# Row maxima, output weights and latent roots placed anew in a hybrid attention and convolution block

## Chip, cores and metric

The kernel runs on one core of a Trainium2 chip. The metric is the device time of one execution in microseconds; the median of the runs counts. Engines are named TensorE (PE in the profile, its weight load PEld), VectorE (DVE), ScalarE (ACT), GpSimd (POOL) and SyncE (SP, which only issues transfers).

## What is computed

One layer of a streaming encoder on 1024 frames of width 1024, with 16 meta tokens ahead of them, and a final norm:

```
n = RMSNorm(h);  z = n @ W_in  ->  conv value | conv gate | c_q (384) | c_kv (256) | k_rot (32)
A: u = a * sigmoid(gate); causal depthwise conv, 31 taps; LayerNorm; swish
B: q = RMSNorm(c_q) @ W_uq;  k, v = RMSNorm(c_kv) @ W_ukv;  rotary on q and the shared k_rot;
   8 heads, softmax over visible chunks (64 frames a chunk, causal by chunk)
h += concat(RMSNorm(A), RMSNorm(B)) @ W_out
h += (silu(conv3(n2 @ W_up)) * conv3(n2 @ W_up)) @ W_down,  n2 = RMSNorm(h)
out = RMSNorm(h), meta tokens dropped
```

All of it is in float32. The kernel makes each float32 product from three TensorE products of a high and a low part: a value x is rounded to `hi` (float32r), `lo = x - hi`, and hi*hi + hi*lo + lo*hi are summed.

## The kernel before

The work is traced in one program; a scheduler orders each engine's instructions by a simulated timeline, with earlier traced work first among what is ready. Three kinds of blocks change this order: `manual_schedule` keeps the traced order on the engines named, `issue_after(x)` puts what is traced in it, on the engine of x, behind x, and `high_priority` puts its instructions ahead of others that are ready. Within an engine everything then runs in that order. 43 equal pages of on-chip memory are shared by weights, activations and heads.

Stages, in order of time:

- Norm of the input and its transposition, then the gated unit (`glu`) of the convolution's four channel groups. Each group's 31 taps (`conv31`, lines 300 to 308) run on VectorE as some 50 operations of 513 columns.
- The latents (class `Latent`): `multiply(g)` makes c_kv or c_q for a third of the rows (three tiles, one PSUM bank each) with ScalarE's squares behind it, and `normalize(g)` takes the root (`rsqrt`, line 173: ScalarE's square root, VectorE's reciprocal, one Newton step), scales the banks to `cn`, transposes, and splits into `cH` and `cL` (lines 505, 506). For the latents the Newton step runs on GpSimd (`eng=G`, lines 185 to 196). The key's rotary part is turned on GpSimd within `multiply` (lines 470 to 477), five operations for each third, and is transposed and split within `normalize`. Rotary products of the queries are in `rope` (line 423).
- Weights come through one list (`want`, `load`, `fetch`): SyncE loads `raw`, then `wh` is a copy (line 244 or 246) and `wl` GpSimd's subtraction (line 247). A block of w_out is first scaled by VectorE (line 242).
- `pair(0..3)` makes the queries and keys of two heads each; those of heads 2 to 7 are spilled to DRAM and loaded as heads (`load_head`, ten transfers; the masks are extra rows of `qh` and `kh`). SyncE issues all transfers, in order.
- `max_pass` makes the row maxima of a head: 15 products `smax` (line 645), each reduced by VectorE into `mp`, then one more reduction, a transposition, ScalarE's negated copy `mr` (line 653), and two transfers of it into row RM of `qh` (lines 654, 655). With that row the scores come out of TensorE already shifted.
- Attention runs over 120 units, 15 a head: `score(u)` makes three products and an exponential `p`, its copy `ph` and `pl = p - ph` on GpSimd or VectorE (line 681); `weigh(u)`, four units later, multiplies with the values. At each unit two steps of the next head's `max_pass` are taken, so a head's maxima are made in the first eight units of the head before it. At the first unit of heads 5, 6 and 7 two or three blocks of w_out are fetched. The convolution's LayerNorm (`conv_branch`) is put between, from unit 10 on.
- Then the output projection, the up-projection and the down-projection.

Of the kernel before, what the change touches and what calls it, by code (L numbers as in the profile page):

```python
# [10 lines left out]
F32 = mybir.dt.float32  # L11
# [8 lines left out]
P = 128  # L20
D = 1024
# [72 lines left out]
def block_kernel(ctx: ExitStack, tc: tile.TileContext, a: dict, out: bass.AP):  # L94
# [139 lines left out]
    def fetch(upto, eng=None):  # L234
        while issued[0] < min(upto, len(queue)):
            key, src, shape = queue[issued[0]]
            issued[0] += 1
            load(issued[0])
            raw = raws.pop(key)
            wh, wl = page("wh", shape, F32R), page("wl", shape, F32R)  # L240
            if key[0] == "out":
                V.tensor_scalar(raw, raw, outT[:, key[1]:key[1] + 1], None, ALU.mult)
            if eng is None:
                S.activation(wh, raw, AF.Copy)  # L244
            else:
                eng.tensor_copy(wh, raw)
            G.tensor_tensor(wl, raw, f(wh), ALU.subtract)  # L247
            ready[key] = (wh, wl)
# [174 lines left out]
    def rope(dst, ps, i, n, g):  # L423

        ta = ea("ropea", "ta", [P, g, 2, 16])
        tb = ea("ropeb", "tb", [P, g, 2, 16])
        cb = cosq[:n, i, :].unsqueeze(1).unsqueeze(1).broadcast_to([n, g, 2, 16])
        sb = sinq[:n, i, :].unsqueeze(1).broadcast_to([n, g, 16])
        V.tensor_tensor(ta[:n], ps, cb, ALU.mult)
        V.tensor_tensor(tb[:n, :, 0, :], ps[:, :, 1, :], sb, ALU.mult)  # L430
        V.tensor_tensor(tb[:n, :, 1, :], ps[:, :, 0, :], sb, ALU.mult)
        G.tensor_tensor(dst[:, :, 0, :], ta[:n, :, 0, :], tb[:n, :, 0, :], ALU.subtract)
        G.tensor_tensor(dst[:, :, 1, :], ta[:n, :, 1, :], tb[:n, :, 1, :], ALU.add)

    class Latent:
# [8 lines left out]
        def multiply(self, g, odd):  # L444
# [24 lines left out]
            if self.extra:  # L469
                ta, tb = ea("ropea", "ta", [P, 3, 2, 16]), ea("ropeb", "tb", [P, 3, 2, 16])  # L470
                cb = cosq[:, g0:g1, :].unsqueeze(2).broadcast_to([P, 3, 2, 16])
                sb = sinq[:, g0:g1, :]
                G.tensor_tensor(ta, kr, cb, ALU.mult)
                G.tensor_tensor(tb[:, :, 0, :], kr[:, :, 1, :], sb, ALU.mult)
                G.tensor_tensor(tb[:, :, 1, :], kr[:, :, 0, :], sb, ALU.mult)
                G.tensor_tensor(kr[:, :, 0, :], ta[:, :, 0, :], tb[:, :, 0, :], ALU.subtract)
                G.tensor_tensor(kr[:, :, 1, :], ta[:, :, 1, :], tb[:, :, 1, :], ALU.add)

        def normalize(self, g):
# [7 lines left out]
            rsqrt(r[:, :3], ss[:, :3], 1.0 / w, 3, root=True, eng=G)  # L487
# [4 lines left out]
            for k in range(nk + (1 if self.extra else 0)):  # L492
                rows = P if k < nk else DR
                if g == 0:
                    self.cH.append(page(self.name + "H", [rows, TP], F32R))
                    self.cL.append(page(self.name + "L", [rows, TP], F32R))
                pt = bank("tp")
                for i in range(g0, g1):
                    pos, n = KT[i]
                    src = cns[i - g0][:n, k * P:(k + 1) * P] if k < nk else krall[:n, i].rearrange("p x c -> p (x c)")  # L500
                    transpose(pt[:rows, pos - base:pos - base + n], src, n)
                hi, lo, ps = self.cH[k][:, base:end], self.cL[k][:, base:end], pt[:rows, :end - base]
                if k < nk:
                    gk = latT[:, goff + k:goff + k + 1]
                    S.activation(hi, ps, AF.Copy, scale=gk)
# [37 lines left out]
    def rot(g, odd):  # L543
        rts[g] = rot_multiply(g, odd)


    steps = [
# [3 lines left out]
        lambda: lcq.multiply(2, 1), lambda: lcq.normalize(1), lambda: rot(0, 0),  # L551
# [9 lines left out]
    qmask_d = dram.tile([NMASK, TP], F32, name="qmask_d")  # L561
    kmask_d = dram.tile([NMASK + 1, TP], F32, name="kmask_d")
    SY.dma_start(out=qmask_d, in_=a["qmask"])
# [28 lines left out]
    def load_head(h):  # L592
# [15 lines left out]
        SY.dma_start(out=f(qh)[DN + DR:RM, Q0:T], in_=qmask_d[:, Q0:T])  # L608
# [20 lines left out]
    def max_pass(tiles):  # L629
# [24 lines left out]
        SY.dma_start(out=f(qh)[RM:RM + 1, 16:T], in_=f(mr)[:8])  # L654
        shifts.append(SY.dma_start(out=f(qh)[RM:RM + 1, Q0:16], in_=f(mr)[8:9, :2]).ins)
# [6 lines left out]
    def score(u):  # L662
# [18 lines left out]
        (V if turn[0] % PLV[h] == 0 else G).tensor_tensor(pl[:n], p32[:n], f(ph)[:n], ALU.subtract)  # L681
# [4 lines left out]
    PLV = [4, 4, 4, 3, 3, 2, 2, 2]  # L686
# [82 lines left out]
    def conv_branch():  # L769
        lng = page("lng", [P, D])  # L770
        SY.dma_start(out=lng[:, :DC], in_=a["conv_ln_g"].partition_broadcast(P))
        SY.dma_start(out=lng[:, DC:], in_=a["conv_ln_b"].partition_broadcast(P))
# [285 lines left out]
    fill = iter(())  # L1058
# [258 lines left out]
```

## Time and profile before

| | |
|---|---|
| time, median of 3 runs | 1281.35 us (1278.2 to 1284.28) |
| the profiled execution's own time | 1281.71 us |
| its span, first to last instruction | 1279.9 us |
| mean granted TensorE clock | 0.976 |
| busy: PE, DVE, ACT, POOL | 1199.5, 904.4, 542.1, 333.7 us |

Busy times are sums over the whole span; matmuls overlap each other, so a busy PE is not PE at its peak. A row of a timeline has the start, the duration, engine, line and tiles (out<-in), and in brackets how long the engine was idle before and what ended that. A clock of 1.00 is 2.4 GHz; the other level is 1.2 GHz.

### The profile page before, as it was taken

How to read it: one execution, taken by the hardware profiler on the slowest of the kernel's cores; microseconds unless marked ns; L12 is line 12 of the kernel's file. 1: busy time of each engine (PE TensorE's matmuls, PEld its weight loads, DVE VectorE, ACT ScalarE, POOL GpSimd, SP SyncE). 2: the span in 40 equal slices, each digit the busy share in tenths (PEclk: the TensorE clock that was granted, in tenths of full speed). 3: DMA queues.
4: the chain of work that ended last, by engine and by line, in shares of the span. 5: the costliest groups of instructions: out<-in, count | busy, mean ns of one | idle time of the engine just before them, and what ended most of it. 6: DMA issues, size and time to landing. Idle time of an engine off the chain costs nothing.

```text
span 1279.9 us, 20327 instructions
## 1 busy us (share of the span) xinstructions
PE 1199.5 (94%) x7867; PEld 1105.6 (86%) x7867; DVE 904.4 (71%) x1600; ACT 542.1 (42%) x1049; POOL 333.7 (26%) x309
## 2 busy tenths in 40 slices
PE   7899779988997999997999999999999989999997
PEld 6799678978886778887999999999999968888886
DVE  6799979956878866788878878778787742142134
ACT  7212433346775553344443444434444343333322
POOL 2334573214656700102000000000000055515530
PEclk9899889999999899998999999999999989999999
DMA  7100110485533111232122121221212346636611
GB/s 263 54 26 26 38 50 32 116 246 125 116 96 111 46 54 66 86 136 92 67 83 99 67 83 67 83 98 68 83 67 83 124 132 197 220 129 203 206 74 66
DMA packets 47397, 130.54 MB, mean 102 GB/s; under 512 B 8282, under 2 KB 12954, under 8 KB 47300
## 3 DMA queue, kind: packets, MB, share of 16 engines
q1 hardware_dynamic: 47300, 129.24, 31.6%
q8 instruction: 62, 1.02, 0.3%
q14 instruction: 35, 0.29, 0.1%
HBM read 98.36 MB, written 28.33 MB: 99 GB/s over the span
## 4 chain that ended last, share of the span: by engine, by line
PE 64%; DVE 5%; DMA 2%; ACT 1%; issue 1%; DVEq 0%; SPq 0%; ACTq 0%; POOL 0%
PE up L919 34%; PE pd L162 6%; PE pd L164 6%; PE pd L163 6%; PE po L162 2%; PE po L164 2%; PE po L163 2%; DVE pl L681 1%; DMA raw<-w_out 1%; PE acc L702 1%; PE acc L704 1%; PE po L967 1%; PE st L669 1%; PE acc L703 1%; PE st L670 1%
## 5 line engine op out<-in xcount | busy, mean ns | idle before, releaser
L247 POOL TENSOR_TENSOR wl<-raw,wh 128x1024 fp32r<-128x1024 f32 (+3 forms) x75 | 195.0, 2604 | 636.0 <-ACT wh L244 581.8
L162 PE MATMUL pd<-wh,gp 128*128 128x512 f32 (+1 forms) x356 | 139.0, 397 | 4.2 <-ACT wh L244 2.4
L164 PE MATMUL pd<-wh,gp 128*128 128x512 f32 (+1 forms) x356 | 138.9, 393 | 1.6 <-DVE gp L1140 1.6
L163 PE MATMUL pd<-wl,gp 128*128 128x512 f32 (+1 forms) x356 | 139.7, 393 | 0.0
L1140 DVE TENSOR_TENSOR gp<-gt,gp 128x512 fp32r<-128x512 f32 x44 | 43.6, 995 | 127.1 <-ACT gp L1139 127.0
L681 POOL TENSOR_TENSOR pl<-p,ph 128x320 fp32r<-128x320 f32 (+11 forms) x76 | 80.1, 1059 | 78.0 <-ACT ph L679 46.0
L1128 ACT ACTIVATE tg<-row,ffnw 128x1024 f32<-128x1024 f32 x44 | 52.3, 1237 | 110.4 <-DVE row L953 110.4
L162 PEld LDWEIGHTS pd<-wh,gp 128*128 128x128 f32 x356 | 67.9, 191 | 20.5 <-ACT wh L244 2.8
L164 PEld LDWEIGHTS pd<-wh,gp 128*128 128x128 f32 x356 | 67.5, 190 | 17.3 <-DVE gp L1140 2.0
L163 PEld LDWEIGHTS pd<-wl,gp 128*128 128x128 f32 x356 | 67.4, 189 | 14.9
L919 PE MATMUL up<-xT2h,uw 128*128 128x258 f32 (+1 forms) x352 | 72.6, 285 | 4.3 <-ACT xT2h L167 4.3
L1129 DVE SCALAR_TENSOR_TENSOR tg<-row,ffnw,tg 128x1024 f32<-128x1024 f32 x44 | 54.6, 1282 | 29.5 <-ACT tg L1128 29.5
L919 PE MATMUL up<-xB11h,uw 128*128 128x258 f32 (+1 forms) x352 | 72.2, 282 | 0.0
L673 ACT ACTIVATE p<-st 128x320 f32<-128x320 f32 (+11 forms) x120 | 53.4, 455 | 44.1 <-DVE pl L681 17.2
L919 PE MATMUL up<-xT1h,uw 128*128 128x258 f32 (+1 forms) x352 | 72.0, 285 | 0.0
L1139 ACT ACTIVATE gp<-gt 128x512 fp32r<-128x512 f32 x44 | 27.7, 630 | 104.5 <-DMA gt<-gated_d 96.2
L919 PE MATMUL up<-xT3h,uw 128*128 128x258 f32 (+1 forms) x352 | 71.5, 283 | 0.0
L919 PE MATMUL up<-xB21h,uw 128*128 128x258 f32 (+1 forms) x352 | 71.3, 283 | 0.0
L919 PE MATMUL up<-xT4h,uw 128*128 128x258 f32 (+1 forms) x352 | 70.2, 282 | 0.0
L919 PE MATMUL up<-xB22h,uw 128*128 128x258 f32 (+1 forms) x352 | 70.0, 282 | 0.0
L244 ACT ACTIVATE wh<-raw 128x1024 fp32r<-128x1024 f32 (+2 forms) x66 | 65.8, 1006 | 4.2 <-DMA raw<-w_uqn 3.5
L646 DVE TENSOR_REDUCE mp<-smax 128x1 f32<-128x264 f32 (+9 forms) x120 | 53.7, 475 | 18.6 <-PE smax L645 17.9
(286 smaller groups left out, 3748.7 us busy)
## 6 DMA issues: line engine op xcount, KB each, us to landing
raw<-w_up SPq DMA_DIRECT2D x44, 512.0 KB
raw<-w_down SPq DMA_DIRECT2D x44, 512.0 KB
gated_d<-tg SPq DMA_DIRECT2D x22, 512.0 KB
gt<-gated_d SPq DMA_DIRECT2D x44, 256.0 KB
raw<-w_ag SPq DMA_DIRECT2D x8, 512.0 KB
raw<-w_out SPq DMA_DIRECT2D x8, 512.0 KB
ht<-x SPq DMA_DIRECT2D x8, 512.0 KB
h_d<-ht SPq DMA_DIRECT2D x8, 512.0 KB
```

Source lines behind the costliest of these rows:

```text
L162: PE.matmul(ps, lhsT=wh, rhs=xh, start=(first and i == 0), stop=False)
L163: PE.matmul(ps, lhsT=wh, rhs=xl, start=False, stop=False)
L164: PE.matmul(ps, lhsT=wl, rhs=xh, start=False, stop=(last and i == n - 1))
L244: S.activation(wh, raw, AF.Copy)
L247: G.tensor_tensor(wl, raw, f(wh), ALU.subtract)
L646: anchor[0] = V.tensor_reduce(mp[:n, 3 * j + pc:3 * j + pc + 1], ps[:n, :k1 - k0], AX.X, ALU.max).ins
L673: S.activation(p32[:n], ps[:n, :w], AF.Exp, scale=SCALE)
L681: (V if turn[0] % PLV[h] == 0 else G).tensor_tensor(pl[:n], p32[:n], f(ph)[:n], ALU.subtract)
L919: PE.matmul(ps[:, :self.w], lhsT=wt[:, wj, k], rhs=x[:, k], start=(fresh and k + j == 0), stop=(k == 3 and j == 2), skip_group_check=True)
L1128: S.activation(tg, row[:, 2:2 + SEQ], AF.Identity, scale=ffnw[:, m, 2:3], bias=ffnw[:, m, 3:4])
L1129: V.scalar_tensor_tensor(tg, row[:, 1:1 + SEQ], ffnw[:, m, 1:2], tg, ALU.mult, ALU.add)
L1140: V.tensor_tensor(gp[:, 1], src, f(gp)[:, 0], ALU.subtract)
```

## The change

1. `fetch`: for w_out ScalarE makes `wh` with the scale in it, and VectorE makes `wl` from raw, scale and `wh` in one operation. GpSimd and the separate scaling go. The fetches in heads 5 to 7 no longer name an engine.
2. `rope` and the low parts in `Latent.normalize` get high priority on VectorE.
3. The root of the latents runs wholly on VectorE, in traced order and with high priority.
4. The key's rotation is done once for all nine tiles (`turn_keys`), behind `lkv.normalize(2)`; its transposition and split move behind `lcq.normalize(1)` (`spread_keys`).
5. `lng`, the convolution norm's constants, is loaded right behind the latents' steps, not in `conv_branch`. A row of zeros joins `qmask_d`, and row RM of `qh` is loaded with it.
6. The two transfers of `mr` are issued by ScalarE.
7. One `pl` in four is VectorE's in every head; before it was one in four in heads 0 to 2, one in three in 3 and 4, one in two in 5 to 7.
8. A head's 18 steps (16 used) of `max_pass` are spread evenly over 15 units, starting five units before the head ahead of it begins; those of head 1 over the first ten units of head 0.

```diff
@@ fetch
+            ready[key] = (wh, wl)
             if key[0] == "out":
-                V.tensor_scalar(raw, raw, outT[:, key[1]:key[1] + 1], None, ALU.mult)
+                g = outT[:, key[1]:key[1] + 1]
+                S.activation(wh, raw, AF.Copy, scale=g)
+                V.scalar_tensor_tensor(wl, raw, g, f(wh), ALU.mult, ALU.subtract)
+                continue
@@ rope
-        V.tensor_tensor(ta[:n], ps, cb, ALU.mult)
...
+        with tc.high_priority():
+            V.tensor_tensor(ta[:n], ps, cb, ALU.mult)
...
@@ Latent.multiply
-            if self.extra:
-                ta, tb = ea("ropea", "ta", [P, 3, 2, 16]), ea("ropeb", "tb", [P, 3, 2, 16])
...
-                G.tensor_tensor(ta, kr, cb, ALU.mult)
...
@@ Latent.normalize
-            rsqrt(r[:, :3], ss[:, :3], 1.0 / w, 3, root=True, eng=G)
+            with tc.high_priority(), tc.manual_schedule(engines={mybir.EngineType.DVE}):
+                rsqrt(r[:, :3], ss[:, :3], 1.0 / w, 3, root=True)
...
+                with tc.high_priority():
                     V.scalar_tensor_tensor(lo, ps, gk, f(hi), ALU.mult, ALU.subtract)
-                else:
-                    split_ps(hi, lo, ps)
+
+    def turn_keys():
+
+        t = page("kt", [P, 2, 9, 2, 16])
+        ta, tb = t[:, 0], t[:, 1]
+        G.tensor_tensor(ta, krall, cosq.unsqueeze(2).broadcast_to([P, 9, 2, 16]), ALU.mult)
+        G.tensor_tensor(tb[:, :, 0, :], krall[:, :, 1, :], sinq, ALU.mult)
...
+    def spread_keys():
...
+            pt = bank("tp")
...
+            split_ps(hi[:, base:end], lo[:, base:end], pt[:DR, :end - base])
@@ steps
+    lng = page("lng", [P, D])
+    zrow = page("zrow", [1, TP])
+    G.memset(zrow, 0.0)
...
-        lambda: lcq.multiply(2, 1), lambda: lcq.normalize(1), lambda: rot(0, 0),
+        lambda: lcq.multiply(2, 1), lambda: lcq.normalize(1), spread_keys, lambda: rot(0, 0),
...
+        if i == 6:
+            turn_keys()
+
+    SY.dma_start(out=lng[:, :DC], in_=a["conv_ln_g"].partition_broadcast(P))
+    SY.dma_start(out=lng[:, DC:], in_=a["conv_ln_b"].partition_broadcast(P))
...
+    SY.dma_start(out=qmask_d[NMASK:], in_=zrow)
@@ load_head
-        SY.dma_start(out=f(qh)[DN + DR:RM, Q0:T], in_=qmask_d[:, Q0:T])
+        SY.dma_start(out=f(qh)[DN + DR:RM + 1, Q0:T], in_=qmask_d[:, Q0:T])
@@ max_pass
-        SY.dma_start(out=f(qh)[RM:RM + 1, 16:T], in_=f(mr)[:8])
-        shifts.append(SY.dma_start(out=f(qh)[RM:RM + 1, Q0:16], in_=f(mr)[8:9, :2]).ins)
+        S.dma_start(out=f(qh)[RM:RM + 1, 16:T], in_=f(mr)[:8])
+        shifts.append(S.dma_start(out=f(qh)[RM:RM + 1, Q0:16], in_=f(mr)[8:9, :2]).ins)
@@ score
-        (V if turn[0] % PLV[h] == 0 else G).tensor_tensor(pl[:n], p32[:n], f(ph)[:n], ALU.subtract)
+        (V if turn[0] % PLV == 0 else G).tensor_tensor(pl[:n], p32[:n], f(ph)[:n], ALU.subtract)
...
-    PLV = [4, 4, 4, 3, 3, 2, 2, 2]
+    PLV = 4
@@ the stream of units
+    LEAD, PIECES = 5, 18
+    per = len(stream) // H
+    pieces = {}
+    for h in range(1, H):
...
+            g = (k * (per - LEAD)) // PIECES if h == 1 else per * (h - 1) - LEAD + (k * per) // PIECES
+            pieces.setdefault(g, []).append(h)
...
-                fill = max_pass(slots[h + 1]) if h + 1 < H else iter(())
                 if h >= 5:
-                    fetch(at[("out", 0)] + (2, 5, 8)[h - 5], V)
+                    fetch(at[("out", 0)] + (2, 5, 8)[h - 5])
             score(u)
-            next(fill, None)
-            next(fill, None)
+            for k in pieces.get(g, ()):
+                if k not in passes:
+                    passes[k] = max_pass(slots[k])
+                next(passes[k], None)
```

## Rows read from the trace of the kernel before

**Rows 1.** Busy time by stretch: length, PE, PEld, DVE, ACT, POOL, PEclk, DMA, GB/s.

```profile
60.00:276.00 216.00, 195.02 (x1221) 187.95 (x1220) 196.31 (x304) 68.76 (x156) 92.34 (x120) 0.96 0.24 68
120.00:180.00 60.00, 43.44 (x267) 41.67 (x267) 49.85 (x75) 17.47 (x44) 36.17 (x33) 0.89 0.14 43
276.00:301.00 25.00, 17.84 (x113) 16.34 (x113) 10.39 (x23) 14.21 (x31) 9.82 (x15) 0.93 0.86 216
301.00:382.00 81.00, 76.91 (x549) 69.77 (x549) 68.27 (x169) 59.94 (x146) 43.46 (x64) 0.98 0.41 94
382.00:455.00 73.00, 61.76 (x394) 52.84 (x395) 61.01 (x107) 44.11 (x115) 48.49 (x37) 0.93 0.27 85
```

**Rows 2.** Timeline of PE: four waits, and the score of unit 10 of head 0.

```profile
143.80 0.61 PE L162 MATMUL pc<-wh,nH 128*128 128x288 f32 x1 [8.76 <-ACT cn L490]
...
170.01 0.61 PE L163 MATMUL pc<-wl,nH 128*80 128x384 f32 x1 [7.16 <-POOL wl L247]
...
278.98 0.34 PE L669 MATMUL st<-qh,kh 116*80 116x322 f32 x1 [3.42 <-DMA qh<-mr]
...
292.21 0.31 PE L669 MATMUL st<-qh,kh 116*128 116x320 f32 x1
...
300.97 0.53 PE L669 MATMUL st<-qh,kh 116*80 116x322 f32 x1 [4.18 <-DMA qh<-mr]
```

**Rows 3.** Timeline of ACT: second latent root, and the maxima of head 0.

```profile
132.44 0.30 ACT L178 ACTIVATE t<-ss,epst 128x3 f32<-128x3 f32 x1
143.27 1.20 ACT L490 ACTIVATE cn<-pc,r 128x256 f32<-128x256 f32 x3 [10.54 <-POOL r L196]
...
267.66 0.25 ACT L653 ACTIVATE mr<-mt 9x128 fp32r<-9x128 f32 x1
```

**Rows 4.** Timeline of DVE: the reciprocal of the first latent root.

```profile
127.78 0.16 DVE L179 RECIPROCAL r<-t 128x3 f32<-128x3 f32 x1
```

**Rows 5.** Timeline of POOL: two splits of weights.

```profile
160.54 9.41 POOL L247 TENSOR_TENSOR wl<-raw,wh 128x768 fp32r<-128x768 f32 x1
...
412.63 2.34 POOL L247 TENSOR_TENSOR wl<-raw,wh 128x1024 fp32r<-128x1024 f32 x1
```

**Rows 6.** Instructions by tile, `raw` of w_out: count, least, median and greatest ns.

```profile
L247 POOL TENSOR_TENSOR wl<-raw,wh x8: 2337/2384/2787, 392.4 to 442.1; 128x1024 fp32r<-128x1024 f32 x8
```

**Rows 7.** Timeline of SyncE's queue: issue, and the issuing time.

```profile
275.82 0.74 SPq L654 DMA_DIRECT2D qh<-mr  x1
...
287.89 0.28 SPq L608 DMA_DIRECT2D qh<-qmask_d  x1
...
297.01 0.66 SPq L655 DMA_DIRECT2D qh<-mr  x1
```

**Rows 8.** Groups of DVE by line, 382 to 455 us: busy, mean ns | idle before.

```profile
L681 DVE TENSOR_TENSOR pl<-p,ph 128x320 fp32r<-128x320 f32 (+11 forms) x25 | 26.4, 1063 | 6.8 <-ACT ph L679 5.9 <-PE acc L704 0.2
...
L246 DVE CAST wh<-raw 128x1024 fp32r<-128x1024 f32 x8 | 7.1, 891 | 0.1
L242 DVE TENSOR_SCALAR raw<-raw,outT 128x1024 f32<-128x1024 f32 x8 | 6.1, 765 | 0.4 <-DMA raw<-w_out 0.4
```

**Rows 9.** Groups of DVE by line, 301 to 382 us.

```profile
L681 DVE TENSOR_TENSOR pl<-p,ph 128x320 fp32r<-128x320 f32 (+9 forms) x18 | 10.3, 571 | 4.6 <-ACT ph L679 3.6 <-PE acc L704 0.7
```

**Rows 10.** Timeline of DVE in head 6.

```profile
411.86 3.52 DVE L681 TENSOR_TENSOR pl<-p,ph 80x384 fp32r<-80x384 f32 x1
```

**Rows 11.** The page's costliest groups, whole span.

```profile
L681 POOL TENSOR_TENSOR pl<-p,ph 128x320 fp32r<-128x320 f32 (+11 forms) x76 | 80.1, 1059 | 78.0 <-ACT ph L679 46.0
...
L1129 DVE SCALAR_TENSOR_TENSOR tg<-row,ffnw,tg 128x1024 f32<-128x1024 f32 x44 | 54.6, 1282 | 29.5 <-ACT tg L1128 29.5
...
L673 ACT ACTIVATE p<-st 128x320 f32<-128x320 f32 (+11 forms) x120 | 53.4, 455 | 44.1 <-DVE pl L681 17.2
...
L244 ACT ACTIVATE wh<-raw 128x1024 fp32r<-128x1024 f32 (+2 forms) x66 | 65.8, 1006 | 4.2 <-DMA raw<-w_uqn 3.5
```

**Rows 12.** The chain that ended last, 380 to 390 us: start, length, what.

```profile
382.75 6.08 DMA raw<-w_out
```

More of the change, by code (lines that the diff above doesn't have):

```diff
@@ L247, in fetch @@
             G.tensor_tensor(wl, raw, f(wh), ALU.subtract)
-            ready[key] = (wh, wl)
     def weight(key, ahead=3):
@@ L491, in normalize @@
             nk = w // P
-            for k in range(nk + (1 if self.extra else 0)):
-                rows = P if k < nk else DR
+            for k in range(nk):
                 if g == 0:
-                    self.cH.append(page(self.name + "H", [rows, TP], F32R))
-                    self.cL.append(page(self.name + "L", [rows, TP], F32R))
+                    self.cH.append(page(self.name + "H", [P, TP], F32R))
+                    self.cL.append(page(self.name + "L", [P, TP], F32R))
                 pt = bank("tp")
@@ L499, in normalize @@
                     pos, n = KT[i]
[L500 to L505, printed above, removed]
-                    V.scalar_tensor_tensor(lo, ps, gk, f(hi), ALU.mult, ALU.subtract)
-                else:
-                    split_ps(hi, lo, ps)
+                    transpose(pt[:, pos - base:pos - base + n], cns[i - g0][:n, k * P:(k + 1) * P], n)
+                hi, lo, ps = self.cH[k][:, base:end], self.cL[k][:, base:end], pt[:, :end - base]
+                gk = latT[:, goff + k:goff + k + 1]
+                S.activation(hi, ps, AF.Copy, scale=gk)
+                with tc.high_priority():
+                    V.scalar_tensor_tensor(lo, ps, gk, f(hi), ALU.mult, ALU.subtract)
+    def turn_keys():
[3 more added lines that the diff above has]
+        G.tensor_tensor(tb[:, :, 0, :], krall[:, :, 1, :], sinq, ALU.mult)
+        G.tensor_tensor(tb[:, :, 1, :], krall[:, :, 0, :], sinq, ALU.mult)
+        G.tensor_tensor(krall[:, :, 0, :], ta[:, :, 0, :], tb[:, :, 0, :], ALU.subtract)
+        G.tensor_tensor(krall[:, :, 1, :], ta[:, :, 1, :], tb[:, :, 1, :], ALU.add)
+    def spread_keys():
+        hi, lo = page("kvH", [DR, TP], F32R), page("kvL", [DR, TP], F32R)
+        kvH.append(hi)
+        kvL.append(lo)
+        for g0, g1 in KG:
+            base, end = KT[g0][0], KT[g1 - 1][0] + KT[g1 - 1][1]
+            pt = bank("tp")
+            for i in range(g0, g1):
+                pos, n = KT[i]
+                transpose(pt[:DR, pos - base:pos - base + n], krall[:n, i].rearrange("p x c -> p (x c)"), n)
+            split_ps(hi[:, base:end], lo[:, base:end], pt[:DR, :end - base])
     lkv, lcq = Latent("kv", KL, 3, DR), Latent("cq", QL, 2, 0)
@@ L1057, in block_kernel @@
     SIDE = [10 + 3 * i for i in range(10)] + [40 + 4 * i for i in range(10)]
-    fill = iter(())
+    LEAD, PIECES = 5, 18
+    per = len(stream) // H
+    pieces = {}
+    for h in range(1, H):
+        gen = {}
+        for k in range(PIECES):
+            g = (k * (per - LEAD)) // PIECES if h == 1 else per * (h - 1) - LEAD + (k * per) // PIECES
+            pieces.setdefault(g, []).append(h)
+    passes = {}
     for g in range(len(stream) + LAG):
```

17 lines of the change are left out of this document (4 added, 13 removed).

## Prediction

> **What bounds the kernel now.** I read the busy time by stretch first. TensorE is the engine that sets the end: the change touches nothing behind attention's end at about 455 us, so the question is where TensorE stands idle ahead of that, and for whom. In 120 to 180 us it works 43.44 of 60 us, in 276 to 301 it works 17.84 of 25, and in 382 to 455 (the last three heads of attention) 61.76 of 73; the stretch 301 to 382, with heads of the same shape, loses only 4.1 of 81 [rows 1]. These are 16.6, 7.2 and 11.2 us of idle time. The granted clock in the three is 0.89, 0.93 and 0.93, which can hide at most another 6.6, 1.8 and 5.1 us of half-speed running; part of that falls into the idle time.
>
> Next, TensorE's timeline, for the waits themselves. Two waits fill the first stretch: 8.76 us for ScalarE's copy `cn` and 7.16 us for GpSimd's `wl`. Two more, 3.42 and 4.18 us, are waits of the first score of heads 0 and 1 for the transfer of the negated row maxima [rows 2].
>
> Then the engine that each wait names, in its own timeline. ScalarE takes the square root of the second latent group at 132.44 and stands until 143.27 for `r`, 10.54 us [rows 3]; that `r` comes from GpSimd's five tiny operations, behind the key rotation in its queue. The first group's reciprocal, on VectorE, came only at 127.78 [rows 4], between convolution taps. The 7.16 us wait stands on one GpSimd subtraction of 768 columns that took 9.41 us [rows 5], where 1024 columns elsewhere take 2.38 [rows 6].
>
> For the maxima: ScalarE has `mr` of head 0 at 267.66 + 0.25 [rows 3], and SyncE's queue issues its transfer at 275.82, 7.9 us later, behind spills [rows 7]. For the last heads: VectorE's `pl` takes 1063 ns a time there, x25 [rows 8], against 571 ns in the heads before, x18 [rows 9]. One of them, at 411.86, took 3.52 us [rows 10], and GpSimd split a block of w_out from 412.63 on for 2.34 us [rows 5]. ScalarE's exponentials wait 17.2 us in all for `pl` [rows 11].
>
> **The latents' root on VectorE.** It removes GpSimd's five operations for each of six groups and adds four small ones behind the reciprocal on VectorE. The trace has no such chain in this place; the reciprocal beside it takes 0.16 us [rows 4], so 24 more make 3.8 us of VectorE. The root of the first group then follows its square root and no longer stands behind taps, so ScalarE doesn't block, and the second group's `r` is there before TensorE wants the bank: the 8.76 us go. What is late next is `wl`, 7.16 us. The change takes key rotation and roots out of GpSimd's queue in front of it but not the taps beside it; I count a third, 2.4. Of the 6.6 us of clock I count 2. That is 13. The ends are 0 and 23.2 (all idle, all clock). Against the upper end stands VectorE itself: from 60 to 276 us it is busy 196.3 of 216 [rows 1], so with 3.8 more it has 15.9 us to give before the taps hold up the splits. Hence 13, not 20.
>
> **Key rotation in one lump, key spread later, high priority for rotary products and low parts, norm constants loaded early.** I cost them at nothing. The transposes and splits are the same ones; GpSimd has 24 of 60 us free in 120 to 180 [rows 1]. Five operations on 288 columns are at most 3.3 us in one piece, estimated from 2.38 for 1024 [rows 6]; if a weight split queues behind it, that is the price. The high-priority operations run in any case, so taps move back behind them by as much, under TensorE's own work. Two early pages (the constants and the zero row) stand against two key pages taken later; if a weight load lacks its page, the price is a wait like the 7.16.
>
> **The maxima's transfers on ScalarE's queue.** The two per head leave SyncE's queue, where spills and loads stood in front of them. Head 0 can then start when TensorE is done with the values at 275.5: 3.4 us gained. They now cost ScalarE's queue 0.74 + 0.66 us a head, by SyncE's issue times [rows 7]: 11.2 us over eight heads. ScalarE works 44.1 of 73 us in the last heads [rows 1], and scores run four units ahead of their use, so I count 1 of it as lost; without that cover it is all 11.2. The zero row adds one 4 KB transfer to SyncE's queue while that waits anyway; each shift must follow its head's mask load, which landed long before. The block of late spills and head 2's loads is ordered behind the first shift only on the shift's engine, so it is now free to go earlier.
>
> The Trainium skill speaks against a gain here: "DMA: Bandwidth & Descriptors", § Issuing engines are not separate DMA queues, says that issuing from several engines saves only the sequencer's time to initiate a transfer. By that rule head 0 would gain 1.4 us and not 3.4, and the time would be 2 us later. The 7.9 us between `mr` and its issue [rows 3, 7] passed in an in-order queue ahead of any initiation, so I go by the rows.
>
> **Maxima spread over a head.** The count (15 products and reductions a head) stays; from head 2 on they start five units before the preceding head ends its predecessor and end at the same unit. So the load on VectorE per unit falls from two reductions in eight units to about one in all. But head 2's maxima now start at unit 10 of head 0. That unit's score ran at 292.21 [rows 2], while SyncE was held until 297.01 by the landing of head 2's `qmask` rows, issued at 287.89 [rows 7]. So TensorE, in order, may stand 4.8 us there: the 4.18 us of head 1 are gained and given back. Later heads' loads are issued at the start of the head two before them, when the transfers of pairs are over, so I count no wait there. For heads 0 and 1 together I take 3.4 + 1 of clock = 4.4, with ends at -5 (wait in full, no gain) and 9.4.
>
> **w_out without GpSimd; one `pl` in four on VectorE.** Removed: eight GpSimd subtractions of 2.38 us [rows 6], 19.1 us, and VectorE's scaling and cast, 6.1 + 7.1 us [rows 8]. Added: eight VectorE operations of 1024 columns with two inputs at 1.282 us, 10.3 us, and eight ScalarE copies at 1.006 us [rows 11], 8.0 us. Of 45 units in heads 5 to 7, 11 `pl` stay on VectorE, not 25; 14 go to GpSimd at 1.059 us [rows 11], 14.8 us, less than the 19.1 it lost. VectorE's excess in `pl` was 25 x (1063 - 571) ns = 12.3 us. The three heads can give 11.2 us of idle and up to 5.1 of clock; with VectorE like that of the earlier heads they would still lose some 4 us in 73, as 301 to 382 does. I take 11, with ends at 2 and 16.3.
>
> A rule speaks against the new operation: the Trainium skill, "SBUF — State Buffer", § Who interferes with whom, has a VectorE instruction with two SBUF inputs contend with GpSimd's reads. The 3.52 us `pl` agrees. By it the eight new operations would block GpSimd 10.3 us in all, and if all of that showed, the 11 would be 0.7.
>
> **Sum.** 13 + 4.4 + 11 - 1 = 27.4 us. The profiled execution took 1281.71 us, 1279.9 of it span; that gives 1254.3. It stands 0.4 above the median of the three runs, so I predict 1254. Half a per cent, 6.4 us, is about what a measurement of this kernel can tell from no change.
>
> **Rivals.** (1) Only one of the two big terms comes. If VectorE is the bound ahead of attention, the latents' 13 turn into a later wait for splits, and the time is 1267; for it speak the 196.3 of 216 us, against it that taps can run on into 276 to 301, where VectorE works 10.4 of 25 us [rows 1]. If the last heads stay as slow because GpSimd, with three `pl` of four, is late, it is 1265; against that, heads with the same share in 301 to 382 run with 4 us lost. (2) The change doesn't do what it says: the order that the scheduler writes places roots and copies as late as now, or another GpSimd operation starves for 9 us, and the gains cancel: 1281. (3) Slower: ScalarE becomes the engine that waits. Its copies of w_out stand in order ahead of exponentials, and the first w_out block lands 6.08 us after its issue [rows 12]; three heads make 18.2 us, the sixteen issues 11.2. Then the last heads gain nothing and the time is 1281.4 - 13 - 4.4 + 29.4 = 1293. It decides once more than 17.4 of the 29.4 us show. For it: VectorE is held by the same transfer now; against it: ScalarE is free 40% of that stretch and the scheduler may place the copies late.
>
> **Chances.** Forecast (1240 to 1262) 0.52; one term only (1262 to 1273) 0.25; nothing (1275 to 1288) 0.11; slower 0.12. Faster by over 0.5%: 0.77; within: 0.11; slower: 0.12. The best case is 23.2 + 9.4 + 16.3 = 48.9 us, 1232, which would need every idle microsecond; I start the range at 1237 and end it at 1282, leaving out the slower rival, half of the third case and a little below.
>
> **What would show it.** Right: no wait of TensorE for `cn` or `r` in the latents, reciprocals within a microsecond of their root; `mr` issued from ScalarE's queue right behind its copy; no GpSimd `wl` from w_out and `pl` on VectorE near 0.57 us; the up-projection starting some 27 us earlier. Wrong: a wait of TensorE on the maxima of head 2 well over 5 us, ScalarE idle on `raw`, taps running into attention with `sl` late, or a starved GpSimd split of 5 us and more in the latents.

## Result and profile after

The median fell from 1280.18 us (1278.2 to 1284.28, 4 runs) to 1265.31 us (1264.12 to 1267.82, 4 runs), a ratio of 0.9884 with a 95% interval of 0.9861 to 0.9906: 14.9 us faster, about half of the 27 us that I had predicted. The profiled execution took 1265.01 us, its span is 1263.2 us and its mean clock 0.984.

The busy time by stretch, in the columns and stretches of [rows 1]:

```profile
60.00:276.00 216.00, 195.16 (x1219) 187.05 (x1218) 197.87 (x323) 65.14 (x150) 75.67 (x81) 0.98 0.25 69
120.00:180.00 60.00, 50.72 (x315) 47.86 (x315) 59.93 (x97) 19.69 (x50) 19.00 (x11) 0.97 0.14 43
276.00:301.00 25.00, 21.89 (x139) 19.62 (x138) 17.10 (x37) 18.44 (x41) 10.55 (x18) 0.93 0.78 193
301.00:382.00 81.00, 79.14 (x578) 72.11 (x577) 72.28 (x171) 61.64 (x153) 48.95 (x69) 1.00 0.45 102
382.00:455.00 73.00, 69.00 (x448) 59.28 (x447) 47.65 (x106) 55.22 (x134) 35.27 (x38) 0.98 0.26 82
```

From 60 to 276 us TensorE works as long as before, 195.16 us against 195.02. It gained 7.3 us from 120 to 180 and had lost them again by 240: from 120 to 240 us it works 99.16 us, before 99.45. From 276 us on it is busier in every stretch, by 4.1, 2.2 and 7.2 us. So attention has the gain and the latents have none.

Why the latents have none is seen on VectorE. This is its timeline around the first group's root, whose square root ScalarE had finished at 117.48 + 0.30:

```profile
127.99 0.17 DVE L179 RECIPROCAL r<-t 128x3 f32<-128x3 f32 x1
128.07 0.14 DVE L185 TENSOR_SCALAR v<-ss 128x3 f32<-128x3 f32 x1
128.12 0.75 DVE L311 SCALAR_TENSOR_TENSOR acc<-d,convw,acc 128x513 f32<-128x513 f32 x1
128.78 0.75 DVE L305 SCALAR_TENSOR_TENSOR acc<-u,convc,acc 128x513 f32<-128x513 f32 x1
...
130.52 0.15 DVE L190 TENSOR_TENSOR t<-r 128x3 f32<-128x3 f32 x1
...
132.59 0.15 DVE L191 TENSOR_TENSOR t<-t,v 128x3 f32<-128x3 f32 x1
...
134.65 0.16 DVE L193 SCALAR_TENSOR_TENSOR r<-t,r 128x3 f32<-128x3 f32 x1
```

The reciprocal comes where it came before [rows 4], and between most of the steps that follow it stand three taps and more, 0.75 us each: five operations of 0.15 us took 6.8 us. In the other groups they took 3.0 to 9.5 us. So the first group's `r` is complete at 134.81, later than in the kernel before, where ScalarE could use it at 130.41:

```profile
130.41 1.19 ACT L490 ACTIVATE cn<-pc,r 80x256 f32<-80x256 f32 x3 [11.29 <-POOL r L196]
```

VectorE itself hardly waits any more. In the kernel before it was busy 109.43 of the 120 us from 120 to 240, now 118.17 (its row stands with e7 below):

```profile
120.00:240.00 120.00, 99.45 (x625) 95.64 (x625) 109.43 (x179) 43.31 (x101) 63.64 (x80) 0.93 0.13 39
```

What it gained went to the taps. The last of them, in the kernel before and in the changed kernel:

```profile
250.62 0.75 DVE L308 SCALAR_TENSOR_TENSOR acc<-d,convw,acc 128x513 f32<-128x513 f32 x1
...
239.75 0.75 DVE L311 SCALAR_TENSOR_TENSOR acc<-d,convw,acc 128x513 f32<-128x513 f32 x1
```

The taps are through 10.9 us earlier, and their results are wanted only in `conv_branch`, from unit 10 of attention on. ScalarE's timeline in the changed kernel shows who waits for `r`, and a new wait further down:

```profile
134.84 0.47 ACT L486 ACTIVATE cn<-pc,r 80x256 f32<-80x256 f32 x1 [12.01 <-DVE r L193]
...
164.83 1.20 ACT L486 ACTIVATE cn<-pc,r 128x256 f32<-128x256 f32 x3 [7.69 <-DVE r L193]
...
269.68 0.25 ACT L677 ACTIVATE mr<-mt 9x128 fp32r<-9x128 f32 x1
276.01 1.24 ACTq L678 DMA_DIRECT2D qh<-mr  x1
278.06 0.61 ACTq L679 DMA_DIRECT2D qh<-mr  x1
278.72 3.02 ACT L167 ACTIVATE vH<-pv 128x512 fp32r<-128x512 f32 x6 [8.79 <-DMA qh<-mr]
281.75 1.28 ACT L697 ACT_TABLE_LOAD   x1
```

The transfer of head 0's maxima now stands in ScalarE's queue and is issued at 276.01, no earlier than SyncE issued it [rows 7]; meanwhile six copies of values and the table load for the exponential wait behind it, 8.79 us. On TensorE the 8.76 and 7.16 us of [rows 2] are gone, and others have come:

```profile
165.36 0.56 PE L157 MATMUL tp<-ident,cn 128*128 128x128 f32 x2 [5.12 <-ACT cn L486]
...
208.67 0.46 PE L157 MATMUL tp<-ident,krall 128*32 128x128 f32 x3 [3.33 <-DVE cqL L500]
...
219.23 0.55 PE L157 MATMUL tp<-ident,cn 128*128 128x128 f32 x3 [4.34 <-DVE acc L309]
227.65 0.62 PE L157 MATMUL tp<-ident,rt 128*128 128x128 f32 x4 [2.37 <-POOL rt L437]
...
280.66 0.35 PE L693 MATMUL st<-qh,kh 116*80 116x322 f32 x1 [3.12 <-DMA qh<-mr]
```

The wait at 219.23 is put down to a tap, but its input `cn` was begun by ScalarE only at 218.59, right behind that group's `r`.

In the last heads VectorE is relieved as meant; its groups by line from 382 to 455 us, against [rows 8]:

```profile
L245 DVE SCALAR_TENSOR_TENSOR wl<-raw,outT,wh 128x1024 fp32r<-128x1024 f32 x8 | 10.9, 1360 | 7.1 <-ACT wh L244 7.1
L705 DVE TENSOR_TENSOR pl<-p,ph 128x320 fp32r<-128x320 f32 (+8 forms) x11 | 8.7, 789 | 4.3 <-PE acc L727 3.6 <-ACT ph L703 0.4
```

For the experiments I cut every profile at three instructions of ScalarE: the table load ahead of the first latent root (the landmark below), the first exponential of attention, and the end of the last copy oT. What lies ahead of the first took 114.3 to 118.2 us and what lies behind the last 821 to 825 us in these profiles, though no part of the change is placed there, so a part of the change is read in the two lengths between. For the kernel before these are 279.66 - 115.66 = 164.0 and 458.50 - 279.66 = 178.8 us. Head 0 is the time from its first exponential to that of head 1.

| kernel | latents to attention | attention | head 0 |
|---|---|---|---|
| before | 164.0 | 178.8 | 22.5 |
| after | 166.9 | 157.9 | 17.2 |
| e1 latents' part alone | 166.0 | 177.4 | 20.6 |
| e2 ScalarE's queue alone | 165.7 | 185.9 | 25.1 |
| e3 spread maxima alone | 163.9 | 172.9 | 25.7 |
| e4 w_out and pl alone | 163.3 | 165.7 | 23.0 |
| e5 after, SyncE's queue | 164.5 | 160.5 | 20.9 |
| e6 after, short root | 160.3 | 159.0 | 16.3 |
| e7 after, few taps | 138.6 | 159.3 | 17.2 |
| e8 e5, last taps late | 149.1 | 167.4 | 30.0 |
| e9 e3 and e4 together | 163.5 | 166.8 | 25.8 |
| e10 e5, last taps half way | 159.4 | 155.5 | 16.8 |
| e11 e5, GpSimd's queue | 164.2 | 166.3 | 23.5 |
| e12 e9, early constants | 163.6 | 167.2 | 25.5 |

One profile can stand some us off the median of its kernel (that of e2 is 5.3 us above it, that of e11 8.3 us), so where a verdict hangs on less, I go by the medians.

### The profile page after: what moved, and what is told of

It reads as the page before. It is cut to its first block, busy times and chain, and to the rows that moved or that the text cites. A ratio compares the mean times of both kernels' runs of the same rounds, so it can differ in the third digit from the quotient of the medians.

```text
span 1263.2 us, 20283 instructions
## 1 busy us (share of the span) xinstructions
PE 1194.7 (95%) x7867; PEld 1102.6 (87%) x7867; DVE 896.3 (71%) x1602; ACT 547.0 (43%) x1057; POOL 310.5 (25%) x276
## 4 chain that ended last, share of the span: by engine, by line
PE 75%; DVE 16%; issue 3%; ACT 2%; DMA 2%; POOL 0%; SPq 0%; DVEq 0%; POOLq 0%; ACTq 0%
PE up L940 35%; PE pd L162 6%; PE pd L164 6%; PE pd L163 6%; DVE acc L305 3%; DVE acc L309 2%; DVE acc L311 2%; PE po L162 2%; PE po L163 2%; PE po L164 2%; PE smax L669 1%; PE st L693 1%; PE st L694 1%; PE st L695 1%; PE acc L728 1%
## 5 line engine op out<-in xcount | busy, mean ns | idle before, releaser
L251 POOL TENSOR_TENSOR wl<-raw,wh 128x1024 fp32r<-128x1024 f32 (+3 forms) x67 | 175.2, 2622 | 671.8 <-ACT wh L248 588.6
L162 PE MATMUL pd<-wh,gp 128*128 128x512 f32 (+1 forms) x356 | 138.6, 396 | 4.2 <-ACT wh L248 2.4
L1171 DVE TENSOR_TENSOR gp<-gt,gp 128x512 fp32r<-128x512 f32 x44 | 47.7, 1091 | 122.3 <-ACT gp L1170 122.1
L705 POOL TENSOR_TENSOR pl<-p,ph 128x320 fp32r<-128x320 f32 (+11 forms) x90 | 92.8, 1045 | 72.2 <-ACT ph L703 50.1
L940 PEld LDWEIGHTS up<-xT2h,uw 128*128 128x128 f32 x352 | 58.2, 192 | 4.5 <-ACT xT2h L167 4.5
```

The costliest lines, as they stand in the source:

```text
L162: PE.matmul(ps, lhsT=wh, rhs=xh, start=(first and i == 0), stop=False)
L705: (V if turn[0] % PLV == 0 else G).tensor_tensor(pl[:n], p32[:n], f(ph)[:n], ALU.subtract)
L940: PE.matmul(ps[:, :self.w], lhsT=wt[:, wj, k], rhs=x[:, k], start=(fresh and k + j == 0), stop=(k == 3 and j == 2), skip_group_check=True)
L1171: V.tensor_tensor(gp[:, 1], src, f(gp)[:, 0], ALU.subtract)
```

## Experiments

**Each part alone.** Four kernels, each the kernel before with one part of the change.

```diff
e1:  root, rope, low parts, turn_keys, spread_keys, lng as after (points 2 to 5, without the zero row)
e2: -SY.dma_start(out=f(qh)[RM:RM + 1, 16:T], ...)     +S.dma_start(...)      (both transfers, point 6)
e3: -fill = max_pass(slots[h + 1]) ... next(fill, None) +pieces over 15 units (point 8)
e4:  fetch of w_out and PLV as after (points 1 and 7)
```

> The kernel before with the latents' part of the change alone: root on VectorE, key rotation in one lump, key spread later, rotary products and low parts at high priority, norm constants loaded early. Theory A (VectorE is the bound ahead of attention, taps stand between the steps of each root, so the copies cn come as late as before): attention's first score within 2 us of the 278.98 of before, the whole time within 4 us of the kernel before, VectorE busy 19 and more of every 20 us from 100 to 220. Rival B (the part does bring its 13 us, and in the full change something else, the early pages beside the zero row or the scalar queue, took it away again): attention some 10 to 13 us earlier and the time 1267 to 1271. Rival C (the part costs time, since the root's steps and the high-priority operations push taps that TensorE waits for): 2 to 5 us slower.

> The kernel before with the two transfers of each head's maxima issued from ScalarE's queue, and nothing else changed. Theory A (the in-order queue of SyncE held the transfer of head 0 back by 7.9 us): the two waits of 3.42 and 4.18 us ahead of heads 0 and 1 shrink to under 1 us and the time falls 3 to 6 us. Rival B (a transfer started from another engine saves only the time to initiate it): the waits shrink by 1.4 us and the time by 1 to 2. Rival C (ScalarE's queue pays the issues, 11.2 us over eight heads, and the scores wait for exponentials): 2 to 8 us slower.

> The kernel before with the maxima of a head spread evenly over the head two before it, transfers still on SyncE's queue. Theory A (two reductions a unit in half a head crowd VectorE, so even spacing gives the low parts and the bank back sooner): heads 1 to 4 shorter by 1 to 2 us each, time 4 to 7 us down. Rival B (VectorE has room in these heads and only the waits on the queue matter): time within 2 us of the kernel before. Rival C (head 2's maxima at unit 10 of head 0 wait for its qmask rows): a wait of 4 us and more of TensorE near 292 us and a time 0 to 5 us up.

> The kernel before with w_out cast by ScalarE and split by VectorE instead of GpSimd, and one low part pl in four on VectorE in all heads. Theory A (in the last three heads VectorE and GpSimd held each other up): pl on VectorE near 0.57 us there, heads 5 to 7 shorter by 9 to 12 us together, time 1268 to 1272. Rival B (GpSimd with three pl of four becomes late instead): heads 5 to 7 shorter by 2 to 4 us, time 1277 to 1279. Rival C (ScalarE waits for raw, 6.08 us three times): slower.

Measured against the kernel before: e1 1281.44 us, ratio 0.9997 (0.9979 to 1.0016); e2 1287.68 us, 1.0055 (1.0035 to 1.0075); e3 1273.64 us, 0.9943 (0.9924 to 0.9963); e4 1271.03 us, 0.9920 (0.9892 to 0.9947).

The latents' part alone brings nothing (theory A), though attention began 2 us later, counted from the landmark, where A had it within 2 us of 278.98. The spread brings 7.3 us (A). Of its rival C the wait came, 4.04 us of TensorE up to 297.63, but not the longer time. w_out and pl bring 10.2 us (A); from head 5's first exponential to the end of attention the last three heads take 445.91 - 386.03 = 59.9 us against 74.8 before, which is more than the 9 to 12 us of A, while heads 0 to 4 take 105.8 us against 104.0.

The queue costs 7.0 us (C). The 11.2 us of issuing are not all of it: attention begins 1.7 us later, behind a wait of ScalarE most of which is not issuing. In e2's timeline of ScalarE:

```profile
269.70 0.25 ACT L653 ACTIVATE mr<-mt 9x128 fp32r<-9x128 f32 x1
276.57 1.24 ACTq L654 DMA_DIRECT2D qh<-mr  x1
278.88 0.61 ACTq L655 DMA_DIRECT2D qh<-mr  x1
279.53 3.02 ACT L167 ACTIVATE vH<-pv 128x512 fp32r<-128x512 f32 x6 [9.59 <-DMA qh<-mr]
```

ScalarE had nothing else in its queue, and the transfer was still issued 6.6 us after `mr`. The trace records for each transfer the completion counter that it raises, and it shows for what ScalarE waited. The transfers of SyncE and ScalarE share eight counters in this program, and here ScalarE stood at the counter of the coming transfer until the transfer that had it last had landed, one that another engine had issued. The counter of the transfer at 276.57 was last given to a spill that SyncE issued at 272.39, and the last part of that spill landed at 276.49:

```profile
272.39 1.10 SPq L760 DMA_DIRECT2D ql_d<-sl  x1
```

**The full change with SyncE's queue (e5).** The change with point 6 undone.

```diff
-S.dma_start(out=f(qh)[RM:RM + 1, 16:T], in_=f(mr)[:8])
+SY.dma_start(out=f(qh)[RM:RM + 1, 16:T], in_=f(mr)[:8])
```

> The changed kernel with the maxima's transfers back on SyncE's queue, all else as changed. Theory A (a transfer on ScalarE's queue still waits for the landing of the transfer eight places before it in the program, and makes ScalarE stand for it, so the move only costs): the six copies vH no longer wait 8.79 us in front of head 0, head 0's first exponential comes 1 to 3 us earlier, and the time is 2 to 6 us below the changed kernel, 1259 to 1263. Rival B (with the maxima spread out, ScalarE's queue is cheap and SyncE's is not): within 1.5 us of the changed kernel or above it.

Measured: 1262.48 us, ratio 0.9852 (0.9838 to 0.9867). That is 2.8 us below the changed kernel, as A had it, but the two intervals overlap, and the table shows an exchange: attention starts 2.4 us sooner and then takes 2.6 us longer; head 0 alone takes 3.7 us longer. So within the full change the queue is worth nothing that I can show, either way; the 7 us that it costs alone are not there any more.

**Is it VectorE (e6, e7)?** The changed kernel with the root ended at the reciprocal, and with 30 of 49 operations of each convolution group left out.

```diff
e6: V.reciprocal(r, t)
   +if short: return
e7: -for k in range(15)   +for k in range(5)    (two loops)
    -for k in range(16)   +for k in range(6)
```

> The changed kernel with the latents' root cut to the reciprocal: the four refining operations on VectorE are left out (the result is a little less exact). Theory A (taps stand between the root's steps, 1.5 to 2 us each, so r comes 5.6 to 9.2 us after its reciprocal): ScalarE's waits for r (12.01, 4.49, 7.69, 3.79 us) fall by some 5 us each, TensorE's waits for cn and acc (5.12, 4.34 us) go, and attention starts 4 to 10 us earlier than 280.7. Rival B (VectorE is simply full ahead of attention; what comes earlier there makes something else later): the waits for r fall but attention starts within 3 us of 280.7 and the time within 3 us of the changed kernel.

> The changed kernel with 30 of the 49 operations of each of the four convolution groups left out (120 taps of about 0.66 us, 79 us of VectorE). Theory A (VectorE is the bound ahead of attention): VectorE falls below 15 of 20 us from 120 to 240, TensorE's waits for cn, cqL and acc there go, attention starts 10 to 20 us earlier than 280.7. Rival B (the spills and loads that keep the transfers 0.88 busy from 240 us on, or GpSimd, set the start): attention starts within 4 us of 280.7.

e6 took 1261.35 us, ratio 0.9842 (0.9825 to 0.9858), 4 us below the changed kernel, and attention starts 6.6 us sooner. ScalarE's waits for `r` are 9.65, 6.33 and 6.68 us for the first three groups, not 5 us shorter each as A had it: now the reciprocal itself waits for taps. The steps of the root between taps are thus one part of the loss, the smaller one. The 24 operations left out are themselves up to 3.6 us of VectorE at 0.15 us each, so this run does not tell their own time from the gaps between them.

e7 took 1235.8 us, ratio 0.9637 (0.9613 to 0.9660), and attention starts 28.3 us sooner, more than the 10 to 20 of A. Busy time from 120 to 240 us, first of the changed kernel:

```profile
120.00:240.00 120.00, 99.16 (x616) 93.50 (x616) 118.17 (x210) 42.23 (x100) 48.44 (x46) 0.96 0.12 37
```

and of e7:

```profile
120.00:240.00 120.00, 119.62 (x789) 116.75 (x789) 56.46 (x138) 51.35 (x118) 29.42 (x64) 1.00 0.34 91
```

VectorE goes from 118.17 of 120 us to 56.46, TensorE from 99.16 to 119.62, and its clock from 0.96 to 1.00. As the work runs up to 28 us earlier in e7, these 120 us hold more of it there. Each group's reciprocal now follows its square root within 0.4 us. The spills and loads were no bound (B), since they came sooner by as much. GpSimd's starved split went with the taps too; two of 768 columns that took 9.70 us together in the changed kernel,

```profile
167.24 9.70 POOL L251 TENSOR_TENSOR wl<-raw,wh 128x768 fp32r<-128x768 f32 x2 [6.66 <-ACT wh L248]
```

took 3.64 us in e7:

```profile
151.91 3.64 POOL L251 TENSOR_TENSOR wl<-raw,wh 128x768 fp32r<-128x768 f32 x2 [2.05 <-ACT wh L248]
```

But taps beside a split do not always hold it up. The five splits from 150 to 180 us of the changed kernel, by tile (least, median and greatest ns), with VectorE busy nearly all the time:

```profile
L251 POOL TENSOR_TENSOR wl<-raw,wh x5: 1836/2301/7902, 152.8 to 175.1; 128x768 fp32r<-128x768 f32 x5
```

One took 7.90 us and the other four 1.84 to 2.33. What sets the slow one apart was not found.

**Taps in another place (e8, e10).** On e5, the last group's taps traced later: behind all latent steps (e8), behind the eleventh of them (e10).

```diff
-if c == 2: conv31(3, us[-1])                 (in glu3, ahead of the eighth step)
+conv31(3, us[-1])                            (e8: behind the loop over the steps)
+if i == 10: conv31(3, us[-1])                (e10: in the loop)
```

> The kernel of e5 (maxima's transfers on SyncE) with the last convolution group's taps traced behind the latents' steps instead of in the middle of them, so that they fill VectorE from about 230 us on. Theory A (VectorE full ahead of attention, with 19 us of room from 240 to 281): attention starts 4 to 10 us earlier than in e5, and the time falls by 3 to 10 us below e5. Rival B (the taps run into attention and hold up the low parts and maxima there): what the start gains, heads 0 and 1 lose, within 3 us of e5 or above it.

> The kernel of e5 with the last convolution group's taps traced behind the tenth latent step, half way between e5 and e8, so that they fill VectorE up to the values but not into head 0. Theory A (taps belong in VectorE's idle time from 240 to 281 us; in head 0 they hold up GpSimd's low parts, as in e8, whose head 0 took 30 us): attention starts between e8's 265 and e5's 279, at 268 to 272, head 0 lasts 17 to 21 us, and the time is 2 to 6 us below e8's 1256.4. Rival B (head 0 is long because it starts before the spills and loads are over, wherever the taps are): head 0 again 26 us and longer, time within 2 us of e8 or above.

e8 took 1256.44 us, ratio 0.9807 (0.9783 to 0.9832). Attention starts 15.4 us sooner than in e5, and head 0 loses 9.1 of that, 30.0 us against 20.9. Taps then run beside head 0's low parts; in e8's timeline of GpSimd:

```profile
266.22 9.19 POOL L704 TENSOR_TENSOR pl<-p,ph 80x322 fp32r<-80x322 f32 x5 [11.03 <-ACT ph L702]
...
282.98 3.08 POOL L704 TENSOR_TENSOR pl<-p,ph 128x320 fp32r<-128x320 f32 x1 [5.43 <-ACT ph L702]
```

These are 1.84 us a piece on average and 3.08, where the row of `pl` before has 1059 ns on average [rows 11]; TensorE waits 2.71 us for the second. The granted clock there was 0.77, against 1.00 in e10, so head 0 ran in part at the lower level. Busy time from 265 to 295 us, in e8:

```profile
265.00:295.00 30.00, 23.64 (x123) 20.07 (x123) 22.44 (x43) 14.98 (x34) 16.81 (x14) 0.77 0.48 117
```

and in e10:

```profile
265.00:295.00 30.00, 29.66 (x195) 26.36 (x194) 22.04 (x46) 21.60 (x48) 11.99 (x20) 1.00 0.75 187
```

e10 took 1254.92 us, ratio 0.9796 (0.9758 to 0.9835): 10.4 us below the changed kernel, the fastest that I ran with the whole computation in it. Head 0 takes 16.8 us, so it was the taps (A) and not the early start (B). The start came only 5.0 us sooner than e5's, at 273.74 where A had 268 to 272, and against e8 the gain of 1.5 us, where A had 2 to 6, is within the intervals.

**Two parts together (e9), and one edit more (e12).** e9 is e3 and e4 in one kernel; it differs from e5 by the latents' part and the zero row (I had put it down as the latents' part alone). e12 adds the early loads of the norm constants.

```diff
e12 on e9: lng = page(...) ahead of the steps, its two loads behind them, out of conv_branch
```

> The kernel before with the spread maxima and the w_out part only: latents' part left as before, maxima's transfers on SyncE's queue. It differs from e5 by the latents' part alone. Theory A (the latents' part brings nothing by itself, and the two other parts add up to the whole gain, 7.3 + 10.2 us): 1261 to 1265, within 2 us of e5. Rival B (the latents' part is worth something once attention is faster): 3 us and more above e5.

> The kernel of e9 (spread maxima, w_out part) with one edit of the latents' part: the two loads of the norm constants stand ahead of the spills instead of between head 2's loads and head 1's maxima. Theory A (these two loads are all that the latents' part brought: without them head 1's second transfer no longer waits for the landing of head 2's mask rows): SyncE issues the two transfers of head 1's maxima back to back, 0.8 us apart instead of 3.9, TensorE's wait of 4.0 us near 296 falls to about 1.3, head 0 lasts 20 to 22 us instead of 25.8, and the time is 1263 to 1267, 4 to 8 us below e9. Rival B (the root on VectorE or the late key spread brought it): within 2 us of e9, head 0 still 25 us.

e9 took 1271.36 us, ratio 0.9919 (0.9888 to 0.9949), no better than e4 alone and 8.9 us above e5, so A fell; the gains of e3 and e4 do not add up. Its head 0 takes 25.8 us. e12 took 1268.5 us, ratio 0.9906 (0.9889 to 0.9923), its head 0 25.5 us, so its A fell too: SyncE does issue the two transfers 1 us apart, but TensorE's wait stayed. This wait of TensorE for head 2's loads, at unit 10 of head 0, in e9 (the line names the transfer that had one of their counters next):

```profile
296.39 0.30 PE L648 MATMUL smax<-kh,qh 115*128 115x144 f32 x1 [4.00 <-DMA qh<-mr]
```

in e12:

```profile
297.56 0.46 PE L652 MATMUL smax<-kh,qh 115*128 115x144 f32 x1 [5.49 <-DMA kh<-kmask_d]
```

and in e5:

```profile
293.98 0.30 PE L669 MATMUL smax<-kh,qh 115*128 115x144 f32 x1 [1.31 <-DMA kh<-kmask_d]
```

Between e12 and e5 stand the root, the priorities, the keys and the zero row, and of these the zero row shows in the loads. Without it `qmask` has 19 rows, and a load of 19 rows ran on one of the sixteen DMA engines. Where one stands alone, in e9 from 338.90 to 342.85 us (packets, then the queue's packets, MB and share of 16 engines):

```profile
DMA packets 20, 0.08 MB, mean 20 GB/s; under 512 B 1, under 2 KB 1, under 8 KB 20
...
q1 hardware_dynamic: 20, 0.08, 6.3%
```

and in e5, a load of 20 rows, from 334.85 to 336.20 us:

```profile
DMA packets 31, 0.09 MB, mean 67 GB/s; under 512 B 10, under 2 KB 10, under 8 KB 30
...
q1 hardware_dynamic: 30, 0.08, 18.5%
```

6.3% of sixteen is one engine, for 3.95 us; 18.5% is three at a time on average, and the load with a row more is through in 1.35 us. The Trainium skill has this, in "DMA: Bandwidth & Descriptors", § Why a DMA increments its semaphore by 16 and not by 1: the number of engines is the largest one up to 16 that divides the number of rows, so 19 rows use one and 20 use ten. The trace agrees: 19 rows run on one engine, and 20 rows land in ten parts. Between spills that one engine is far behind, and the eight counters pass its lateness on. SyncE's waits in e9 from 235 to 310 us (engine and line, what ended the wait, us, times, longest):

```profile
SPq L658 <- DMA qh<-qmask_d: 3.2, 1, 3.2
SPq L627 <- DMA qh<-qmask_d: 2.4, 1, 2.4
```

All seven kernels with 19 rows (the kernel before, e1 to e4, e9 and e12) have such waits of 2.0 to 3.6 us; the seven with 20 rows have none above 0.2. The trace also records when each part of a transfer landed. Head 2's `qmask` rows were complete 8.1 to 10.0 us after their issue in the kernels with 19 rows, and 4.6 to 6.6 us after it in those with 20. `kmask`, 20 rows everywhere, is held up with them: of its ten parts in e12 nine had landed by 294.11, and the tenth landed at 297.43, 0.31 us behind the 19 rows of `qmask`. TensorE's wait of 5.49 us ended with that, so some 3.3 us of it are the missing row's.

The row is not all there is to this wait. In e11, described next, the load has 20 rows too. There the mask rows were complete at 295.69, where e5 has 293.84, and TensorE, which came to unit 10 sooner than in e5, still waited for them:

```profile
295.93 0.46 PE L669 MATMUL smax<-kh,qh 115*128 115x144 f32 x1 [4.52 <-DMA kh<-kmask_d]
```

The zero row by itself was not run, so what share of the 6.0 us between e12 and e5 is its, and what the root's, the priorities' and the keys', stays open.

**GpSimd's queue (e11).** e5 with the maxima's transfers issued by GpSimd, whose transfers have other counters.

```diff
-SY.dma_start(out=f(qh)[RM:RM + 1, 16:T], in_=f(mr)[:8])
+G.dma_start(out=f(qh)[RM:RM + 1, 16:T], in_=f(mr)[:8])
```

> The kernel of e5 with the maxima's transfers issued by GpSimd, whose transfers carry no completion counter that a SyncE transfer has used shortly before. Theory A (what held head 0's transfer back was not the order of a queue but the landing of an earlier spill whose completion counter it shares): GpSimd issues it within 1 us of mr at about 267 us, 7 us earlier than SyncE or ScalarE did, the wait of 2 to 4 us of TensorE ahead of head 0 shrinks below 1, and the time is 1 to 4 us below e5. Rival B (the transfers' engines are full of spills, 0.9 busy, and a transfer issued early lands as late): issued early, landed at 277 as before, wait unchanged. Rival C (GpSimd pays for issuing, in front of its low parts): waits of scores for pl in every head, time above e5.

Measured: 1262.44 us, ratio 0.9839 (0.9802 to 0.9875), the time of e5. `mr` was there at 270.49 + 0.25, and GpSimd issued the transfer 0.3 us later:

```profile
271.04 0.70 POOL L678 DMA_DIRECT2D qh<-mr  x1 [3.42 <-ACT mr L677]
```

So the mechanism of A is shown: with the counters out of the way nothing else held the transfer, and TensorE's first score no longer waits for it. The time of A did not come. Attention starts 164.2 us behind the landmark, where e5 has 164.5: ScalarE, with nothing in between, has the last values and its table load to do first:

```profile
278.41 0.59 ACT L167 ACTIVATE vH<-pv 80x512 fp32r<-80x512 f32 x1 [0.80 <-PE pv L164]
279.02 1.28 ACT L697 ACT_TABLE_LOAD   x1
280.32 0.43 ACT L697 ACTIVATE p<-st 80x322 f32<-80x322 f32 x1
```

The wait in front of head 0 had covered these.

## Why the prediction was right, and where it was not

The sign and the range held, but the case that came is not my forecast (1240 to 1262, 0.52); it is the first rival, one of the two big terms only (1262 to 1273, 0.25), in the form in which VectorE is the bound ahead of attention: 1267 forecast there, 1265.31 measured. That the two numbers are so close is luck in part. Without the latents' part and the zero row the kernel takes 1271.36 us (e9), and the rest came mostly from head 0 of attention (25.8 us there, 17.2 in the changed kernel), where the sum had counted on another wait.

**Latents, 13 us: wrong.** The step that failed is "The root of the first group then follows its square root and no longer stands behind taps". The reciprocal still came 10.2 us behind its root, taps stood between the steps that follow, and `r` was complete 4 us later than before. The cap of 15.9 us that VectorE had to give failed with it, and not because the time was missing: of the 19.7 us that VectorE was idle from 60 to 276, 10.6 lay between 120 and 240 (109.43 of 120 busy). The change did fill 8.7 of these, but with taps, which ended 10.9 us earlier and which nothing waits for there, while the chain that TensorE needs stood behind them. That the taps are what stands in the way is shown by leaving them out (e7, attention 28.3 us sooner) and by moving one group of them (e10, 5.0 us sooner and 7.6 us less in time). The 8.76 and 7.16 us went, as said, and turned into later waits, as the rival had it, though not for splits but for `cn`, `cqL` and `rt`. High priority ranks an instruction among those that are ready, and the scheduler put taps between the dependent steps; e6, without the four steps behind the reciprocal, is 4 us faster. Alone the part was worth nothing (e1).

**Maxima, 4.4 us: the sum too small, its parts wrong.** Head 0's 3.4 us did not come. The step that failed is that the 7.9 us "passed in an in-order queue ahead of any initiation, so I go by the rows": outside that queue the transfer stood as long, 6.6 us in e2, for a counter that moves along with it, and with another counter it stood 0.3 us (e11). The rule that I had set against it, that a transfer started from another engine saves only the time to start it, came nearer: 1.4 us by the rule, nothing measured. And even without the wait attention starts no sooner (e11). The 4.8 us for head 2's mask rows at unit 10 were right as a mechanism: 4.04 us in e3, 4.00 in e9. That the full change is spared them comes, as far as the landings tell, in good part from the zero row, which I had costed at one more 4 KB transfer. The spread itself, for which I had counted nothing beyond head 1, gains 7.3 us alone (e3). In the full change heads 0 to 4 take 95.9 us against 104.0.

**w_out and pl, 11 us: right.** The last three heads take 62.0 us against 74.8, 12.8 us less; alone the part gives 10.2 us (e4). `pl` on VectorE takes 789 ns, not 571, of 1063 before. The copy is 1.14 us and VectorE's new operation 1360 ns where I had 1.006 and 1.282. Of the heads in 301 to 382, which I had taken as having the same share, two gave VectorE one `pl` in three. Which of the two edits brings the gain was not tried apart. The rule of a contended port, by which nearly all of the 11 would go, did not come true in the sum.

**ScalarE, 1 us lost; the slower rival.** ScalarE waited for `raw` once, 3.11 us, not three times 6.08, and the last heads did not suffer. Its long wait was the 8.79 us in front of head 0, which I had not foreseen; 2.4 us of it show in the start of attention (after against e5).

**At nothing:** key rotation in one lump took 4.2 us on GpSimd (182.50 to 186.68), where I had at most 3.3, and nobody waited for it. A starved split was in my list of what would show the forecast wrong; it came, one of 7.90 us.

## What to carry to other kernels

Before a chain of small steps is moved to an engine, look at what stands ready in that engine's queue to be put between the steps: VectorE had 10.6 us free in the stretch, and they went to long filler operations and not to the chain, so the wait only changed its name. A transfer that is issued late is not always behind its queue; look at what its completion counter was last used for, and for a transfer that lands late look at the number of its rows. When a kernel has filler work for an engine, try its place as well as the order of the small steps beside it: moving one group of taps gave 7.6 us (e5 to e10), the latents' part alone none (e1).

## What was not expected of the hardware

- A load of 19 rows took 3.95 us on one DMA engine, one of 20 rows 1.35 us on several; a row of zeros made the transfer shorter.
- GpSimd's subtraction of 768 columns took 1.82 us on average beside an idle VectorE (e7, two in 3.64). Beside a busy VectorE in the changed kernel one took 7.90 us and four others 1.84 to 2.33. `pl` of 320 columns took 3.08 us beside taps (e8).
- An engine that issues a transfer stands for as long as that transfer waits for its counter: 8.79 us of ScalarE for a row of 4 KB.
